# Every second gate and up block by seven products of halves, with the sums of weight halves made by accumulating transfers

## The chip, the cores and the metric

The kernel runs on one core of one Trainium2 chip. The metric is the device time of one execution in microseconds (us); lower is better. In the profile PE is TensorE (matmul), PEld its weight loads, DVE is VectorE, ACT is ScalarE, POOL is GpSimd, and SP is the engine that issues most transfers. A letter q behind an engine's name means its queue of instructions that are no work on data.

## The reference

One inference step of one decoder layer, in float32, for 256 prompt tokens and 8 tokens of running sequences, 264 columns in all. The part that matters here is the feed-forward block, which stands before and after a mixing block:

```python
def swiglu(x, wg, wu, wd):
    return (jax.nn.silu(x @ wg) * (x @ wu)) @ wd

h = h + 0.5 * swiglu(rmsnorm(h, norm_ffn1[l]), ffn1_gate[l], ffn1_up[l], ffn1_down[l])
mix, ... = mixing_block(rmsnorm(h, norm_mix[l]), ...)
h = h + mix
h = h + 0.5 * swiglu(rmsnorm(h, norm_ffn2[l]), ffn2_gate[l], ffn2_up[l], ffn2_down[l])
```

The model width is 2048 (16 tiles of 128 in the contraction), the feed-forward width is 5504 (43 blocks of 128 columns for gate and for up). All weights are read from HBM once.

## The kernel before, in words

**Products in halves of precision.** Activations lie transposed: features on the 128 partitions, the 264 tokens along the free side. Every float32 weight tile `wraw` (eight tiles of 128 by 128, 0.5 MB) is loaded by SP and cut in two float16 parts: ScalarE writes `whi` (line 221, function `high`), VectorE writes the rest `wlo` (line 229, function `low`). Each product of a tile of weights is then three matmuls with 264 columns (lines 288 to 290): high by high, high by low, low by high. A product of a whole block of 128 outputs is `product`: 16 tiles, so 48 matmuls. Inside it stands the order of the work, written out by hand: after every eight tiles the next weight tile is fetched and cut (`fetch`, up to five tiles ahead), then one step of a side schedule runs (`prepare_step`), and `tick` runs what was put on the agenda with `at(delta, ...)`, counted in products. Engines run their instructions in the order in which they are written here.

**The two halves of a feed-forward layer.** `ffn` goes through gate and up for blocks 0 to 21, multiplies them to the activations of the down projection, does the down projection with these blocks, and then the same for blocks 22 to 42. An ordinary block is a gate product, its silu, and an up product.

**Blocks by seven.** Some blocks (list `SEVEN`, 11 in the first layer and 12 in the second, every third one) compute gate and up as one product of two-by-two parts: the weights are cut in gate and up and in the first and second half of the contraction, the input in the halves of the contraction and the two halves of the tokens (132 each). Seven products of 8 tiles do the work of eight (the Winograd form), each as three float16 matmuls with 132 columns (line 410). Three products, with weight halves as they are (tile `sa`, three slots), form the first chunk; four, with sums of weight halves (tile `sb`, four slots), form the second (`chunk_by_seven` with c = 0 and 1). They go to three banks p, q, r; afterwards `by_seven` puts gate and up together from them: ScalarE copies one result (`m`, line 756), VectorE does four additions, a check value and the multiplication with the norm (lines 766 to 774), ScalarE the silu (line 777). The input side, sums of halves of the normed input, is made once a layer by `Norm.form` and `form_split` on ScalarE, POOL and VectorE.

**How the weight sums are made.** `prepare` fills the side schedule `steps`, eight steps a block. POOL issues four loads of 0.5 MB a block into `sraw` (line 332; two buffers, each for half of the tiles). Per buffer ScalarE and VectorE cut three halves to `sa`; VectorE makes the sums `ssum` in three instructions (lines 356 to 358), and ScalarE and VectorE cut these to `sb`. In the order of blocks the second chunk stands one ordinary block behind the first.

**Checks.** `watch` keeps a statistic of each ordinary product (tile `stat`, NSTAT columns) and `twins` one of each block by seven; if one is out of bounds, the whole step is run again in another form of float32.

Of the kernel before, what the change touches and what calls it, by code (L numbers as in the profile page):

```python
# [8 lines left out]
F32 = mybir.dt.float32  # L9
# [29 lines left out]
NSTAT = 320  # L39
# [10 lines left out]
SEVEN = {n: list(range(j, 22, 3)) + list(range(22, NFB, 3)) for n, j in (("1", 10), ("2", 7))}  # L50
# [95 lines left out]
def step(ctx: ExitStack, tc: tile.TileContext, a: dict, shared, bad=None):  # L146
# [171 lines left out]
    def prepare(pool, layer):  # L318

        gu = a[f"w{layer}gu"]
        ks = [slice(0, 4), slice(4, 8)]
        raws = [None, None]
        steps.clear()
        step_no[0] = None

        def load(j, c):
            raws[c] = raw = pool.tile([128, 4, 4, 128], F32, tag="raw", name="sraw", bufs=2)
            for g in range(2):  # L330
                blocks = gu[j, g].rearrange("p (s k) m -> p s k m", s=2)
                queue.dma_start(raw[:, 2 * g : 2 * g + 2], blocks[:, :, ks[c], :])  # L332

        def blocks(j, c):
            if c == 0:
                formed[j, 0] = [
                    pool.tile([128, 3, 8, 128], PART, tag=f"sa{i}", name=f"sa{i}")
                    for i in range(2)
                ]
            high(formed[j, 0][0][:, :, ks[c]], raws[c][:, 0:3], sw)  # L340

        def blocks_low(j, c):
            hi, lo = formed[j, 0]
            low(lo[:, :, ks[c]], raws[c][:, 0:3], hi[:, :, ks[c]], sw)

        sums = [None]

        def all_sums(j, c):
            raw = raws[c]
            if c == 0:  # L350
                formed[j, 1] = [
                    pool.tile([128, 4, 8, 128], PART, tag=f"sb{i}", name=f"sb{i}")
                    for i in range(2)
                ]
            sums[0] = s = pool.tile([128, 4, 4, 128], F32, tag="ssum", name="ssum")
            nc.vector.tensor_tensor(s[:, 2], raw[:, 2], raw[:, 3], op=ALU.add)
            nc.vector.tensor_tensor(s[:, 3], s[:, 2], raw[:, 1], op=ALU.subtract)
            nc.vector.tensor_tensor(  # L358
                s[:, 0:2], raw[:, 0:4:2],
                s[:, 3].unsqueeze(1).to_broadcast([128, 2, 4, 128]), op=ALU.subtract,  # L360
            )
            high(formed[j, 1][0][:, :, ks[c]], s, sw)

        def sums_low(j, c):
            hi, lo = formed[j, 1]
            low(lo[:, :, ks[c]], sums[0], hi[:, :, ks[c]], sw)

        for n, j in enumerate(SEVEN[layer]):
            for s, fn, c in (
                (2, blocks, 0), (3, blocks_low, 0), (3, blocks, 1), (4, blocks_low, 1),  # L370
                (5, all_sums, 0), (6, sums_low, 0), (7, all_sums, 1), (8, sums_low, 1),
            ):
                steps.setdefault(8 * n + s - (3 if n == 0 else 0), []).append((fn, j, c))
            for c in range(2):
                s = -4 if n == 0 else 8 * n + (-2, -1)[c]
                steps.setdefault(s, []).append((load, j, c))

    def prepare_step():
        if step_no[0] is not None and step_no[0] < step_end[0]:
            for fn, j, c in steps.get(step_no[0], ()):  # L380
                fn(j, c)
            step_no[0] += 1

    def chunk_by_seven(j, c, x, forms, banks):
# [7 lines left out]
        def form(n):  # L392
# [4 lines left out]
            (p, 1, lambda k: x[k][:, :, left]), (p, 0, lambda k: x[k + 8][:, :, left]),  # L397
            (r, 0, form(3)),
# [1281 lines left out]
```

## Time and profile before

| | |
|---|---|
| time, median of 3 runs | 1814.26 us (1813.57 to 1816.54) |
| profiled execution, first to last instruction (span) | 1812.0 us |
| TensorE busy | 1796.6 us (99%) |
| VectorE busy | 1391.5 us (77%) |
| ScalarE busy | 958.0 us (53%) |
| GpSimd busy | 250.2 us (14%) |
| transfers | 381.34 MB, mean 210 GB/s |
| mean granted TensorE clock | 0.998 |

The profile comes from one execution. What it gives for that execution is its span; the time outside the span is not shown, and the median of the runs stands 2.3 us above it. A row of a group has the line, the engine, the operation, output and inputs with their shapes, the count, then busy time and mean nanoseconds of one, then the idle time before it and what ended it. Rows of the time line have start, length, engine and line. "Landing" is the time from the issue of a transfer until its data are there.

### The profile page before, as it was taken

Reading aid. Unit: us, or ns where it says so; the run is one execution under the profiler, and the core shown is the slowest. Engines: PE = TensorE matmul, PEld = TensorE weight load, DVE = VectorE, ACT = ScalarE, POOL = GpSimd, SP = SyncE. Lnnn points to the kernel's source line nnn. Section 1 sums busy time; section 2 is a strip of 40 time slices with the busy share of each in tenths; the row PEclk is TensorE's granted clock in tenths of the full one; section 3 lists DMA queues with packets and bytes.
Section 4 is the critical chain, followed back from the end, with each engine's and each line's share of the span. In section 5 each row is a group of like instructions: output and inputs, shape, how many; then the busy total and the mean of one; then the engine's idle time right before and its main releaser. Section 6 shows DMA issues by size and latency. Waiting matters only on the chain.

```text
span 1812.0 us, 42493 instructions
## 1 busy us (share of the span) xinstructions
PE 1796.6 (99%) x17920; PEld 1590.5 (88%) x17920; DVE 1391.5 (77%) x2132; ACT 958.0 (53%) x1329; POOL 250.2 (14%) x339
## 2 busy tenths in 40 slices
PE   9999999999999999999999999999999999999997
PEld 7889988899998888888888888889988889999886
DVE  7888985579997667788888766789986459998554
ACT  7664554445554444667566645655554435554442
POOL 0310000000100222222121022410000001010131
PEclk9999999999999999999999999999999999999999
DMA  9765666645654565988887655756567646564663
GB/s 300 251 219 170 218 225 212 202 157 191 217 189 151 187 190 193 307 279 273 282 282 241 221 179 185 253 191 221 190 187 257 199 147 213 193 209 155 190 193 97
DMA packets 118503, 381.34 MB, mean 210 GB/s; under 512 B 14972, under 2 KB 24796, under 8 KB 118304
## 3 DMA queue, kind: packets, MB, share of 16 engines
q1 hardware_dynamic: 95856, 302.29, 51.1%
q0 software_dynamic: 21504, 75.81, 12.4%
q8 instruction: 142, 2.33, 0.5%
q10 hardware_dynamic: 944, 0.45, 0.1%
q14 instruction: 57, 0.47, 0.1%
HBM read 366.72 MB, written 11.78 MB: 209 GB/s over the span
## 4 chain that ended last, share of the span: by engine, by line
PE 98%; DVE 1%; DMA 0%; ACT 0%; issue 0%; SPq 0%; DVEq 0%; ACTq 0%
PE ps L288 28%; PE ps L290 28%; PE ps L289 28%; PE ps L410 12%; PE ps L506 1%; PE ps L624 0%; PE ps L1349 0%; PE ps L1292 0%; PE ps L1247 0%; DMA wraw<-in_w1gu 0%; DVE sq L698 0%; DVE h L918 0%; PE ps L1270 0%; PE ps L1333 0%; PE ps L1271 0%; ACT whi L221 0%
## 5 line engine op out<-in xcount | busy, mean ns | idle before, releaser
L229 DVE SCALAR_TENSOR_TENSOR wlo<-wraw,whi 128x1024 f16<-128x1024 f32 (+2 forms) x600 | 695.2, 1181 | 97.3 <-ACT whi L221 96.9
L221 ACT ACTIVATE whi<-wraw 128x1024 f16<-128x1024 f32 (+2 forms) x600 | 585.0, 1001 | 202.3 <-PE ps L289 166.8
L290 PE MATMUL ps<-x,wlo 128*128 128x264 f16 x1952 | 539.4, 276 | 0.0
L288 PE MATMUL ps<-x,whi 128*128 128x264 f16 x1952 | 539.4, 276 | 0.0
L289 PE MATMUL ps<-x,whi 128*128 128x264 f16 x1952 | 539.4, 276 | 0.0
L289 PEld LDWEIGHTS <-whi 128*128 128x128 f16 x4522 | 442.2, 98 | 66.4
L288 PEld LDWEIGHTS <-whi 128*128 128x128 f16 x4522 | 442.5, 98 | 65.3 <-issue 0.6
L290 PEld LDWEIGHTS <-wlo 128*128 128x128 f16 x4522 | 442.3, 98 | 65.2
L288 PE MATMUL ps<-a,whi 128*128 128x264 f16 (+2 forms) x1418 | 383.3, 273 | 0.0
L289 PE MATMUL ps<-a,whi 128*128 128x264 f16 (+2 forms) x1418 | 383.3, 273 | 0.0
L290 PE MATMUL ps<-a,wlo 128*128 128x264 f16 (+2 forms) x1418 | 383.2, 273 | 0.0
L288 PE MATMUL ps<-xm,whi 128*128 128x264 f16 x896 | 247.6, 276 | 0.0
L289 PE MATMUL ps<-xm,whi 128*128 128x264 f16 x896 | 247.6, 276 | 0.0
L290 PE MATMUL ps<-xm,wlo 128*128 128x264 f16 x896 | 247.6, 276 | 0.0
L221 ACT ACTIVATE sb<-ssum 128x2048 f16<-128x2048 f32 x46 | 87.9, 1910 | 177.3 <-DVE ssum L358 177.3
L410 PEld LDWEIGHTS <-sb 128*128 128x128 f16 x2208 | 128.8, 98 | 0.7
L860 DVE SCALAR_TENSOR_TENSOR h<-ps,h 128x264 f32<-128x264 f32 x62 | 26.8, 432 | 130.5 <-PE ps L290 130.5
L229 DVE SCALAR_TENSOR_TENSOR sb<-ssum,sb 128x2048 f16<-128x2048 f32 x46 | 105.3, 2289 | 6.0 <-ACT sb L221 3.6
L410 PE MATMUL ps<-f,sb 128*128 128x132 f16 x1656 | 99.0, 221 | 0.0
L410 PEld LDWEIGHTS <-sa 128*128 128x128 f16 x1656 | 97.1, 98 | 0.7
L332 POOL DMA_DIRECT2D sraw<-in_w2gu x48 | 34.6, 722 | 420.3 <-issue 382.0
L332 POOL DMA_DIRECT2D sraw<-in_w1gu x44 | 31.7, 723 | 392.5 <-issue 359.3
(256 smaller groups left out, 1665.9 us busy)
## 6 DMA issues: line engine op xcount, KB each, us to landing
wraw<-in_w2gu SPq DMA_DIRECT2D x124, 512.0 KB, 4.6
wraw<-in_w1gu SPq DMA_DIRECT2D x120, 512.0 KB, 4.9
wraw<-in_win SPq DMA_DIRECT2D x112, 512.0 KB, 5.6
wraw<-in_w1d SPq DMA_DIRECT2D x80, 448.0 KB, 4.1
wraw<-in_w2d SPq DMA_DIRECT2D x80, 448.0 KB, 3.8
sraw<-in_w2gu POOLq DMA_DIRECT2D x48, 512.0 KB, 5.3
sraw<-in_w1gu POOLq DMA_DIRECT2D x44, 512.0 KB, 5.3
wraw<-in_wout SPq DMA_DIRECT2D x32, 512.0 KB, 4.8
```

Of the source, the lines that this page charges most:

```text
L221: nc.scalar.activation(dst, src, AF.Copy, scale=scale)
L229: nc.vector.scalar_tensor_tensor(dst, src, scale, hi, op0=ALU.mult, op1=ALU.subtract)
L288: nc.tensor.matmul(ps, wh, xk[:, 0, :], start=first, stop=False)
L289: nc.tensor.matmul(ps, wh, xk[:, 1, :], start=False, stop=False)
L290: nc.tensor.matmul(ps, wl, xk[:, 0, :], start=False, stop=last)
L332: queue.dma_start(raw[:, 2 * g : 2 * g + 2], blocks[:, :, ks[c], :])
L410: nc.tensor.matmul(out, w[:, f, k, :], b(k)[:, part, :], start=(k + term == 0), stop=(k == 7 and term == 2),)
L506: nc.tensor.matmul(ps[j0 + j], w[:, nk * j + k, :], x[k0 + k][:, part, :], start=(k0 + k + n == 0), stop=(k0 + k == KB - 1 and n == 2),)
L860: nc.vector.scalar_tensor_tensor(h[db], ps, 0.5 / (sw * sa[layer]), h[db], op0=ALU.mult, op1=ALU.add)
```

## The change

1. **More blocks by seven**: every second one, 17 in the first layer (8 to 20, then 22 to 40, in steps of two) and 18 in the second (6 to 20, then 22 to 40), 35 for 23. An ordinary block is between any two of them, and its gate product now stands before the second chunk, its up product behind it.
2. **Sums by transfers**: `ssum` and its VectorE instructions go. The buffer holds three half blocks (1.5 MB): the first half of gate, the second half of gate and the first half of up. After the cuts for the first chunk, POOL issues an accumulating transfer that adds the second half of up to two of these slots (S1 and S2); after the cuts of these, one that adds the second half of gate to S2's slot (S3); after the cut of that, one that adds the first half of gate (S4). Each cut is one instruction on ScalarE and one on VectorE, over one or two slots of 1024 elements.
3. **The rhythm**: six steps of the side schedule a block for eight; one step is now also run at the end of each chunk. In the second chunk the product with S4 comes last. During a down projection no steps run.
4. The form of the sums changes some signs: one more small POOL instruction in `Norm.form`, and by_seven's activations are cut with the opposite sign. `NSTAT` is 288 instead of 320.

```diff
-SEVEN = {n: list(range(j, 22, 3)) + list(range(22, NFB, 3)) for n, j in (("1", 10), ("2", 7))}
+SEVEN = {n: list(range(j, 22, 2)) + list(range(22, NFB - 1, 2)) for n, j in (("1", 8), ("2", 6))}
...
+        def upper(j):
+            raws[j] = raw = pool.tile([128, 3, 8, 128], F32, tag="raw", name="sraw", bufs=2)
+            queue.dma_start(raw[:, 2], gu[j, 1][:, 0:8, :])
+            queue.dma_start(raw[:, 1], gu[j, 0][:, 8:16, :])
+        def lower(j):
+            queue.dma_start(raws[j][:, 0], gu[j, 0][:, 0:8, :])
+        def adds(j, slots, g, s):
+            dst, src = raws[j][:, slots], gu[j, g][:, 8 * s : 8 * s + 8, :]
+            n = slots.stop - slots.start
+            if n > 1:
+                src = src.unsqueeze(1).to_broadcast([128, n, 8, 128])
+            queue.dma_start(dst, src, accum_op=ALU.add)
...
+        def cut(j, c, slots, of):
+            hi, lo = tiles(j, c)
+            high(hi[:, slots], raws[j][:, of], sw)
+        def cut_rest(j, c, slots, of):
+            hi, lo = tiles(j, c)
+            low(lo[:, slots], raws[j][:, of], hi[:, slots], sw)
+        one, two, three_ = slice(0, 1), slice(1, 3), slice(2, 3)
         for n, j in enumerate(SEVEN[layer]):
-            for s, fn, c in (
-                (2, blocks, 0), (3, blocks_low, 0), (3, blocks, 1), (4, blocks_low, 1),
-                (5, all_sums, 0), (6, sums_low, 0), (7, all_sums, 1), (8, sums_low, 1),
+            for s, fn, *what in (
+                (-3, upper), (-2, lower),
+                (0, cut, 0, two, two), (1, cut_rest, 0, two, two), (1, adds, two, 1, 1),
+                (1, cut, 0, one, one), (2, cut_rest, 0, one, one),
+                (4, cut, 1, two, two), (4, cut_rest, 1, two, two), (4, adds, three_, 0, 1),
+                (6, cut, 1, slice(3, 4), three_), (6, cut_rest, 1, slice(3, 4), three_),
+                (6, adds, three_, 0, 0),
+                (8, cut, 1, one, three_), (8, cut_rest, 1, one, three_),
             ):
-                steps.setdefault(8 * n + s - (3 if n == 0 else 0), []).append((fn, j, c))
...
+                steps.setdefault(6 * n + s, []).append((fn, j, *what))
...
             work = (
-                (q, 0, lambda k: x[k][:, :, right]), (q, 2, form(1)), (q, 1, form(0)),
-                (p, 2, form(2)),
-            )
+                (1, q, 2, form(1)), (2, q, 1, form(0)), (3, p, 2, form(2)),
+                (0, q, 0, lambda k: x[k][:, :, right]),
+            )
...
+        prepare_step()
...
-                    elif j - 2 in sevens:
-                        order += [("seven", i - 2, j - 2, 1), ("one", i, j, 0)]
+                    elif j - 1 in sevens:
+                        order += [("gate", i, j, 0), ("seven", i - 1, j - 1, 1), ("up", i, j, 0)]
```

More of the change, by code (lines that the diff above doesn't have):

```diff
@@ L322, in prepare @@
         gu = a[f"w{layer}gu"]
-        ks = [slice(0, 4), slice(4, 8)]
-        raws = [None, None]
+        raws, parts = {}, {}
         steps.clear()
         step_no[0] = None
[L328 to L337, printed above, removed]
+        def upper(j):
+            raws[j] = raw = pool.tile([128, 3, 8, 128], F32, tag="raw", name="sraw", bufs=2)
+            queue.dma_start(raw[:, 2], gu[j, 1][:, 0:8, :])
+            queue.dma_start(raw[:, 1], gu[j, 0][:, 8:16, :])
@@ new lines, in lower, with tiles @@
+        def lower(j):
[6 more added lines that the diff above has]
+            queue.dma_start(dst, src, accum_op=ALU.add)
+        def tiles(j, c):
+            if (j, c) not in formed:
+                formed[j, c] = [
+                    pool.tile([128, 3 + c, 8, 128], PART, tag=f"s{'ab'[c]}{i}", name=f"s{'ab'[c]}{i}")
@@ L821, in ffn @@
                             by_seven(j, i)
+                        continue
+                    if kind != "one":
+                        (gate if kind == "gate" else up)(i, j)
                         continue
```

77 lines of the change are left out of this document (28 added, 49 removed).

## The prediction

> **What bounds the kernel now.** I read the page first (shares of the engines), then the chain of waits that ended last, then one stretch of the gate and up blocks instruction by instruction, then the transfers.
>
> ```profile
> span 1812.0 us, 42493 instructions
> PE 1796.6 (99%) x17920; PEld 1590.5 (88%) x17920; DVE 1391.5 (77%) x2132; ACT 958.0 (53%) x1329; POOL 250.2 (14%) x339
> PE 98%; DVE 1%; DMA 0%; ACT 0%; issue 0%; SPq 0%; DVEq 0%; ACTq 0%
> ```
>
> TensorE carries 98% of the chain: less matmul work is less time, as long as nothing else makes it wait. The chain in order of time (start, length) gives the prices; x72 is the first chunk of a block by seven, x96 its second.
>
> ```profile
> 391.93 4.14 PE ps L410 x72
> 406.87 5.52 PE ps L410 x96
> 423.19 4.14 PE ps L410 x72
> ```
>
> Between the end of a first chunk (391.93 + 4.14 = 396.07) and the second (406.87) lies one ordinary block: 10.80 us, so 5.40 for its gate and 5.40 for its up product. A block by seven costs 4.14 + 5.52 = 9.66 us; one of its products is 5.52 / 4 = 1.38. Each of the twelve blocks that change kind (23 become 35) saves 1.14 us of TensorE: **-13.7 us** in all. That is the whole gain.
>
> The same three blocks as a window (busy time of each engine, granted clock, DMA share, GB/s), and the end of the run:
>
> ```profile
> core 0: us, PE busy (x) PEld busy (x) DVE busy (x) ACT busy (x) POOL busy (x), PEclk, DMA share, GB/s
> 391.93:423.19 31.26, 31.26 (x363) 28.44 (x361) 28.55 (x39) 16.63 (x20) 2.88 (x5) 1.00 0.61 203
> ...
> 1800.00:1812.00 12.00, 0.95 (x12) 0.62 (x12) 4.50 (x14) 0.91 (x4) 0.00 (x0) 0.64 0.42 120
> ```
>
> TensorE has no gap there, VectorE is at 28.55 / 31.26 = 91%, ScalarE at 53%, the DMA engines at 61%.
>
> **What stays beside other work.**
>
> ```profile
> L229 DVE SCALAR_TENSOR_TENSOR wlo<-wraw,whi 128x1024 f16<-128x1024 f32 x420 | 509.5, 1229 | 51.9 <-ACT whi L221 51.7
> L358 DVE TENSOR_TENSOR ssum<-sraw,ssum 128x1024 f32<-128x1024 f32 x46 | 56.3, 1225 | 1.6
> L357 DVE TENSOR_TENSOR ssum<-ssum,sraw 128x512 f32<-128x512 f32 x46 | 31.8, 692 | 1.6
> L356 DVE TENSOR_TENSOR ssum<-sraw 128x512 f32<-128x512 f32 x46 | 31.5, 686 | 0.0
> L664 POOL TENSOR_TENSOR form_t<-form_b x16: 732/747/1385, 46.3 to 1174.6; 128x264 f32<-128x264 f32 x16
> L666 POOL TENSOR_TENSOR form_t<-form_t,form_b x16: 462/960/1329, 47.6 to 1178.0; 128x132 f32<-128x132 f32 x16
> ```
>
> The three sums leave VectorE: 56.3 + 31.8 + 31.5 = 120 us, none of it on the chain, so worth nothing by itself. In the new rhythm, one block by seven and one ordinary block (10.80 + 9.66 = 20.46 us; a "pair" below), VectorE has the old 28.55 less 2 x (1.225 + 0.692 + 0.686) = 5.2 of sums and less about 7 for the ordinary block that goes (four cuts of 1.23 and some 2 us around them): 16.3 of 20.46, 80%. It gets lighter, ScalarE hardly changes, neither becomes the bound. The input forms are now made one a product instead of one in 1.25 to 1.5; their POOL work, 0.75 + 0.96 + two small ones, stays under 4 us in 5.40: hidden, nothing. The negated sign, the smaller statistics tile and the halves of an ordinary block as two calls cost no instruction.
>
> POOL now issues six transfers for a block by seven instead of four, and three of these wait for VectorE. Behind a waiting one, only the loads of the next blocks queue. Bytes for a pair: four ordinary tiles, three half blocks loaded and four added, eleven times 0.5 MB, 5.8 MB in 20.46 us, or 282 GB/s against 203.
>
> **What lies on the path.** The sums S3 and S4 are made in place: the transfer for S3 may start only when VectorE has finished its cut of S2 from the same bytes, that for S4 only when S3 is cut. So per block two accumulating transfers, two hops to POOL and three cuts stand in series, and the first cut is behind the previous block's end. These rows price that series (first ScalarE, VectorE and POOL in order of time, then two summaries):
>
> ```profile
> 407.37 1.47 ACT L221 ACTIVATE sa<-sraw 128x1536 f16<-128x1536 f32 x1
> 408.74 1.04 ACT L221 ACTIVATE whi<-wraw 128x1024 f16<-128x1024 f32 x1
> 409.69 1.47 ACT L221 ACTIVATE sa<-sraw 128x1536 f16<-128x1536 f32 x1
> ...
> 412.42 0.27 ACT L756 COPY m<-ps 128x132 f32<-128x132 f32 x1 [0.52 <-PE ps L410]
> 415.23 0.42 ACT L777 ACTIVATE tb<-y 128x264 f32<-128x264 f32 x1 [2.53 <-DVE y L774]
> 415.55 1.99 ACT L221 ACTIVATE whi<-wraw 128x1024 f16<-128x1024 f32 x2
> 421.75 1.91 ACT L221 ACTIVATE sb<-ssum 128x2048 f16<-128x2048 f32 x1 [4.21 <-DVE ssum L358]
> ```
>
> ```profile
> 389.17 1.22 DVE L358 TENSOR_TENSOR ssum<-sraw,ssum 128x1024 f32<-128x1024 f32 x1
> ...
> 408.87 1.76 DVE L229 SCALAR_TENSOR_TENSOR sa<-sraw,sa 128x1536 f16<-128x1536 f32 x1
> 413.19 0.43 DVE L767 TENSOR_TENSOR y<-ps,y 128x264 f32<-128x264 f32 x1
> 422.34 1.22 DVE L229 SCALAR_TENSOR_TENSOR wlo<-wraw,whi 128x1024 f16<-128x1024 f32 x1
> 423.70 2.29 DVE L229 SCALAR_TENSOR_TENSOR sb<-ssum,sb 128x2048 f16<-128x2048 f32 x1
> ...
> 390.95 1.44 POOL L332 DMA_DIRECT2D sraw<-in_w1gu  x2 [130.47 <-issue]
> 398.94 1.44 POOL L332 DMA_DIRECT2D sraw<-in_w1gu  x2 [6.55 <-issue]
> ```
>
> ```profile
> sraw<-in_w1gu POOLq DMA_DIRECT2D x44, 512.0 KB, 5.3
> cs<-in_c POOLq DMA_DIRECT2D x16, 512.0 KB, 5.9
> out_c_s<-cs POOLq DMA_DIRECT2D x16, 512.0 KB, 5.1
> DMA to landing us min/median/max: 4.3/5.3/12.3
> DMA to landing us min/median/max: 3.2/5.3/8.9
> GB/s 63 189 267 356 383 414 325 231 231 194 47 204 241 398 414 325 346 89 31 173 341 189 215 225 273 273 278 47 0 0 0 0 68 231 309 84 136 267 252 16
> ```
>
> The two landing rows are those of sraw and of cs, 0.5 MB each from POOL. I now follow one turn of the loop, with zero at the end of a second chunk E (412.39 in the rows).
>
> - The result of the block: in the new order its last product touches only one bank, so the copy m and the first of VectorE's sums can go before E. VectorE's second sum (413.19) starts about 0.1 after E, and the silu follows it as in the rows, 415.23 - 413.19 = 2.04 later: silu at 2.1.
> - ScalarE works in program order: silu to next start 0.32 (415.55 - 415.23), a weight cut 0.95 (409.69 - 408.74), then the cut of S1 and S2, which has the size of the sb row, 1.91: ends at 5.3.
> - VectorE's rest of it, 0.04 later as in the rows (421.75 + 1.91 = 423.66, then 423.70), 2.29: 7.6.
> - POOL issues the transfer 0.56 after VectorE ends (389.17 + 1.22 = 390.39, then 390.95): 8.2. It lands L later.
> - S3: cut 1.04 and rest 0.04 + 1.22, hop 0.56, transfer L. S4: cut 1.04, rest 0.04 + 1.22.
>
> Together 8.2 + 2.86 + 2.30 = 13.4, plus 2 L. TensorE wants S4 for the last product of the next second chunk, which without a stall starts at 5.40 (up) + 4.14 (first chunk) + 5.40 (gate) + 3 x 1.38 = 19.08. (That it waits for the slot alone and not the whole tile, I take from the rows: at 409.69 ScalarE writes the second half of sa while VectorE still reads the first, 408.87 to 410.63.) **The stall of a pair is 2 L - 5.7**; the loop has slack only for L under 2.85 us.
>
> L for an accumulating transfer of 0.5 MB is not in the trace. The nearest row is sraw: same queue, bytes and direction, median 5.3, fastest 4.3; the fastest transfer of that size into or out of cs, also from POOL, is 3.2. Reading the destination too adds something between nothing and another whole transfer (out_c_s, which reads such a tile out of the same memory, 5.1): 10.4. I stay near sraw: one more pass of 0.5 MB at the best rate of the row (414 GB/s) is 1.3 us, and half of it is 0.65, because the engines may overlap it: L = 5.9, between 5.3 and 6.6. The stall is then 6.1 us a pair.
>
> It does not come in every pair. After each first half the down projection lets the sums catch up, so 16 of 17 pairs in the first layer and 17 of 18 in the second pay; the first pair of a layer follows no result by seven and pays some 1.5 less. 33 x 6.1 - 3 = **+198 us**.
>
> The clock: in the last 12 us above TensorE has 0.95 us of work and the mean clock is 0.64; if it falls from 1 to 0.5 after t, t + 0.5 (12 - t) = 7.7 gives t = 3.4 us, with almost no work in them. A stall of 6 us is longer. At half clock the last product takes 1.38 more; what comes behind it has the slack of the stall. So between 0 and 33 x 1.38 = 45; I take the middle, **+23**, as no row shows how soon the clock returns. The Trainium skill ("TensorE: Matmul & The Clock Gate", Part 1) says that an idle window of some 3.4 us halves the clock until a busy window has passed; the drop at the end agrees, no run here shows the return, and by that rule the sum would take the whole 45.
>
> Sum against the profiled execution's span of 1812.0: -13.7 + 198 + 23 = +207, 2019 us; the median of the runs is 2.3 above that span, so 2021, and I say **2020**.
>
> **The rivals.**
>
> *The loop closes in time* (faster). Decides at L under 2.85 us. Then only -13.7 is left: 1800.6. For it: the DMA engines are at 61% and some loads on the other queue are quick. Against: no 0.5 MB from POOL landed in under 3.2, and these carry extra work. 0.07.
>
> *The fixed cost rules L*: each lands as the fastest transfer of cs, 3.2; the stall is 0.7, 33 x 0.7 - 3 - 13.7 = +6, 1821. The median rows speak against it. 0.08 up to 1840. The Trainium skill ("DMA: Bandwidth & Descriptors", "Anatomy of one DMA — SWDGE (gpsimd) path") has about 2.0 us plus bytes over 436 GB/s, which for 0.5 MB is 3.2 as an estimate; the fastest cs agrees, the median of sraw, 5.3, does not.
>
> *The DMA engines are the bound.* If an added byte counts twice, a pair is 5.8 + 2.1 = 7.9 MB. At the window's own rate, 203 / 0.61 = 333 GB/s, that is 23.6 us, 3.2 over 20.46: 35 x 3.2 - 13.7 = +98, 1912. For it: 282 GB/s is above the present mean. Against: bursts of 414, at which it would be 19.0 and fit; and the loop above is longer anyhow. 0.07.
>
> *TensorE waits for the whole tile of sums* at the chunk's start: the loop is 13.4 + 5.52 + 2 L against 20.46, the stall 2 L - 1.5 = 10.3, 33 x 10.3 - 3 + 23 - 13.7 = +346, 2160. The bank of m hints at it (the copy waited until E for a slot finished one chunk earlier); the overlapping halves of sa speak against. 0.08.
>
> **How the numbers follow.** The loop with slots and L from 4.3 to 8 has 0.70: by the same formula L = 4.3 gives a stall of 2.9, +79 without the clock, 1893; L = 7.9 (two more passes, 5.3 + 2.6) gives 10.1 and with the whole clock +362, 2176. The range 1850 to 2180 takes in the DMA rival and the whole-tile one at 5.9; outside are the faster case, the 3.2 case and L beyond 8. A measurement here can tell about 0.2% (3.6 us) from no change. Faster 0.07, within 0.2% 0.03 (L just around 2.9 to 3.1), slower 0.90.
>
> **What the new profile would show.** TensorE's chunks of 4.14 and the first three quarters of the second as before, then a gap of about 6 us ahead of the last quarter, released by VectorE's rest of S4; ScalarE waiting for a transfer into sraw twice a pair; POOL's accumulating issues 0.56 after VectorE; a pair at some 27 us instead of 20.46; PEclk under 1.00 in these windows; down projection and mixing block unchanged. Wrong if TensorE has no gap in second chunks, if the transfers land in under 3 us, if the gap stands at the chunk's start (whole tile), or if it is spread over ordinary weight tiles (DMA bound).

## The result

The changed kernel takes 2106.14 us (median of 4 runs, 2104.65 to 2108.55) against 1813.91 (4 runs, 1813.34 to 1816.54): ratio 1.1613, 95% interval 1.1596 to 1.1629. The profiled execution's span is 2106.7 us against 1812.0, so +294.7. The page of the changed kernel (in its rows the matmuls by seven have line 403 for 410, the copy `m` 753 for 756, the accumulating transfers 340, a block's loads 329, 330 and 333):

```profile
span 2106.7 us, 44342 instructions
PE 1876.8 (89%) x18784; PEld 1653.6 (78%) x18784; DVE 1339.2 (64%) x2053; ACT 1004.2 (48%) x1376; POOL 363.5 (17%) x473
PEclk9988889998888999999999999888889998988999
PE 40%; DMA 26%; issue 12%; DVE 11%; ACT 8%; POOL 1%; DVEq 0%; SPq 0%; ACTq 0%; POOLq 0%
```

TensorE's share of the chain fell from 98% to 40%; transfers, VectorE and ScalarE took its place, and TensorE, still the busiest engine, is at 89%. What TensorE waited for (total us, times, longest), in the view of waits:

```profile
PE ps L403 <- ACT sb L221: 172.3, 36, 7.2
PE ps L403 <- DVE sb L229: 37.3, 42, 2.0
```

That is 210 us, all ahead of parts of `sb`, the sums; ordinary weight tiles do not appear. The windows place it by stage:

```profile
core 0: us, PE busy (x) PEld busy (x) DVE busy (x) ACT busy (x) POOL busy (x), PEclk, DMA share, GB/s
90.00:330.00 240.00, 191.97 (x2085) 170.83 (x2084) 146.28 (x193) 106.75 (x122) 39.47 (x52) 0.88 0.78 212
430.00:706.00 276.00, 220.10 (x2577) 198.36 (x2575) 162.27 (x212) 113.17 (x129) 40.65 (x52) 0.88 0.75 190
330.00:430.00 100.00, 100.00 (x891) 86.97 (x890) 50.14 (x66) 40.83 (x42) 0.00 (x0) 1.00 0.63 202
706.00:1300.00 594.00, 592.28 (x5208) 513.61 (x5209) 444.67 (x811) 341.37 (x586) 126.07 (x179) 1.00 0.69 229
```

The down projection (330 to 430) and the mixing block (706 to 1300) keep TensorE busy all but 1.7 us, at clock 1.00. The stages with blocks by seven have TensorE busy 80% of the time at clock 0.88. One pair in the time line, of PE, ACT, DVE and POOL:

```profile
1491.79 4.30 PE L403 MATMUL ps<-f,sb 128*128 128x132 f16 x72
1492.86 0.85 POOL L340 DMA_DIRECT2D sraw<-in_w2gu  x1 [7.36 <-DVE sb L229]
1493.61 2.28 DVE L229 SCALAR_TENSOR_TENSOR sa<-sraw,sa 128x2048 f16<-128x2048 f32 x1
...
1496.20 1.19 POOL L340 DMA_DIRECT2D sraw<-in_w2gu  x1 [2.48 <-DVE sa L229]
1498.79 1.06 ACT L221 ACTIVATE sb<-sraw 128x1024 f16<-128x1024 f32 x1 [2.85 <-DMA sraw<-in_w2gu]
1499.90 0.40 PE L403 MATMUL ps<-x,sb 128*128 128x132 f16 x2 [3.81 <-ACT sb L221]
...
1501.16 2.60 PE L403 MATMUL ps<-x,sb 128*128 128x132 f16 x22 [0.86 <-DVE sb L229]
...
1507.86 1.91 ACT L221 ACTIVATE sb<-sraw 128x2048 f16<-128x2048 f32 x1 [0.62 <-DMA sraw<-in_w2gu]
1509.80 2.29 DVE L229 SCALAR_TENSOR_TENSOR sb<-sraw,sb 128x2048 f16<-128x2048 f32 x1 [2.90 <-ACT sb L221]
1512.39 0.87 POOL L340 DMA_DIRECT2D sraw<-in_w2gu  x1 [9.83 <-DVE sb L229]
```

Three quarters of the second chunk (x72) run, then TensorE stands for 3.81 us until ScalarE has cut S4 (1498.79), runs two matmuls, and waits again, 0.86 us, for VectorE's rest. The gap is where the prediction put it. Below, A1, A2 and A3 are a block's three accumulating transfers in order: here A3 of one block (1492.86), A1 of the next (1496.20) and its A2 (1512.39). The chain of waits through the same pair:

```profile
1484.07 6.15 DMA sraw<-in_w2gu
...
1490.24 1.07 ACT sb L221
...
1492.47 0.69 DVE wlo L229
...
1493.61 2.29 DVE sa L229
...
1496.20 11.56 DMA sraw<-in_w2gu
...
1507.86 1.92 ACT sb L221
...
1509.80 2.31 DVE sb L229
...
1512.39 6.13 DMA sraw<-in_w2gu
```

No TensorE is in it. From one A2 (1484.07) to the next (1512.39) are 28.32 us: the landing of A2, the cut of S3, the rests that stand behind it in VectorE's order, the next block's A1 with 11.56, the cut of S1 and S2, A2 again. This is a second closed loop, and the prediction did not have it.

A1 in the second layer (median landing at the end of the row), the landing of all accumulating transfers, large and small (minimum, median, maximum), and GpSimd's queue as a share of 16 engines:

```profile
sraw<-in_w2gu POOLq DMA_DIRECT2D x18, 1024.0 KB, 10.4
DMA to landing us min/median/max: 5.5/6.4/12.0
q0 software_dynamic: 42976, 156.03, 31.2%
```

### The profile page after: what moved, and what is told of

It reads as the page before. It is cut to its first block, busy times and chain, and to the rows that moved or that the text cites. A ratio compares the mean times of both kernels' runs of the same rounds, so it can differ in the third digit from the quotient of the medians.

```text
span 2106.7 us, 44342 instructions
## 1 busy us (share of the span) xinstructions
PE 1876.8 (89%) x18784; PEld 1653.6 (78%) x18784; DVE 1339.2 (64%) x2053; ACT 1004.2 (48%) x1376; POOL 363.5 (17%) x473
## 3 DMA queue, kind: packets, MB, share of 16 engines
q0 software_dynamic: 42976, 156.03, 31.2%
## 4 chain that ended last, share of the span: by engine, by line
PE 40%; DMA 26%; issue 12%; DVE 11%; ACT 8%; POOL 1%; DVEq 0%; SPq 0%; ACTq 0%; POOLq 0%
DMA sraw<-in_w2gu 14%; PE ps L288 12%; PE ps L289 12%; PE ps L290 12%; DMA sraw<-in_w1gu 12%; ACT sb L221 4%; DVE sb L229 4%; DVE sa L229 3%; ACT whi L221 2%; DVE wlo L229 1%; ACT sa L221 1%; PE ps L403 1%; DMA wraw<-in_w1gu 1%; PE ps L500 1%; DVE y L771 1%
## 5 line engine op out<-in xcount | busy, mean ns | idle before, releaser
L229 DVE SCALAR_TENSOR_TENSOR wlo<-wraw,whi 128x1024 f16<-128x1024 f32 (+2 forms) x552 | 634.2, 1178 | 156.5 <-ACT whi L221 155.8
L288 PEld LDWEIGHTS <-whi 128*128 128x128 f16 x4138 | 412.0, 100 | 64.8 <-issue 0.6
L289 PEld LDWEIGHTS <-whi 128*128 128x128 f16 x4138 | 411.2, 99 | 65.4 <-issue 0.3
L288 PE MATMUL ps<-x,whi 128*128 128x264 f16 x1568 | 450.3, 287 | 0.0
L289 PE MATMUL ps<-x,whi 128*128 128x264 f16 x1568 | 448.4, 286 | 0.0
L290 PE MATMUL ps<-x,wlo 128*128 128x264 f16 x1568 | 446.6, 285 | 0.0
L403 PEld LDWEIGHTS <-sb 128*128 128x128 f16 x3360 | 235.7, 110 | 228.0 <-ACT sb L221 178.9
L229 DVE SCALAR_TENSOR_TENSOR sb<-sraw,sb 128x1024 f16<-128x1024 f32 (+1 forms) x105 | 166.0, 1581 | 299.9 <-ACT sb L221 299.9
L403 PE MATMUL ps<-x,sb 128*128 128x132 f16 x840 | 101.8, 309 | 192.3 <-ACT sb L221 163.6
L221 ACT ACTIVATE sb<-sraw 128x1024 f16<-128x1024 f32 (+1 forms) x105 | 140.6, 1339 | 261.2 <-DMA sraw<-in_w2gu 132.8
L403 PE MATMUL ps<-f,sb 128*128 128x132 f16 x2520 | 157.5, 224 | 17.4 <-DVE sb L229 8.7
L403 PEld LDWEIGHTS <-sa 128*128 128x128 f16 x2520 | 147.7, 98 | 3.4 <-DVE sa L229 2.3
## 6 DMA issues: line engine op xcount, KB each, us to landing
sraw<-in_w2gu POOLq DMA_DIRECT2D x18, 1024.0 KB, 10.4
```

The source lines that it names most:

```text
L221: nc.scalar.activation(dst, src, AF.Copy, scale=scale)
L229: nc.vector.scalar_tensor_tensor(dst, src, scale, hi, op0=ALU.mult, op1=ALU.subtract)
L288: nc.tensor.matmul(ps, wh, xk[:, 0, :], start=first, stop=False)
L289: nc.tensor.matmul(ps, wh, xk[:, 1, :], start=False, stop=False)
L290: nc.tensor.matmul(ps, wl, xk[:, 0, :], start=False, stop=last)
L403: nc.tensor.matmul(out, w[:, f, k, :], b(k)[:, part, :], start=(k + term == 0), stop=(k == 7 and term == 2),)
```

## The experiments

Between two copies `m`, that is from one result by seven to the next, the kernel before takes 31.26 us (three blocks, "a triple"), the changed one 28.93 in the mean of 31 (two blocks, "a pair"; 20.46 without a gap). This distance is the measure in what follows. The ratios are to the kernel before.

**1. Every third block again, sums still by transfers.** `SEVEN` as before; ten steps a block, and the chain of a block laid wholly behind that of the block before.

```diff
-                (-3, upper), (-2, lower),
-                (0, cut, 0, two, two), (1, cut_rest, 0, two, two), (1, adds, two, 1, 1),
+                (-6, upper), (-5, lower),
+                (-3, cut, 0, two, two), (-2, cut_rest, 0, two, two), (-2, adds, two, 1, 1),
...
-                (6, adds, three_, 0, 0),
-                (8, cut, 1, one, three_), (8, cut_rest, 1, one, three_),
+                (4, adds, three_, 0, 0),
+                (7, cut, 1, one, three_), (7, cut_rest, 1, one, three_),
```

> The sums stay accumulating transfers, with the same bytes and the same in-place order for a block, but the blocks by seven go back to every third one (23 of them) and the chain of a block is spread over the ten steps that three blocks have (first transfer three steps, second three, third three before its use). Theory 1 (the loop of dependent transfers is too long for the rhythm): three blocks last 31.3 us, more than the loop's 28, so TensorE has no gaps and the time is that of the kernel before, 1810 to 1818. Theory 2 (the DMA engines are the bound): eight ordinary tiles, three loads and four added half blocks in 31.3 us, at the rates of the changed kernel about 0.65 of the engines, also no gaps: 1810 to 1820. Theory 3 (an accumulating transfer costs time wherever it stands, through POOL or memory): 23/35 of the loss stays, about +200, 2010.

Measured: 1983.18 us (1982.32 to 1989.43), ratio 1.0946 (1.0928 to 1.0964); a triple 38.29. The expectation of no gaps missed. With this step table the series A1, A2, A3 and the next block's cuts follow one another in a circle of 38 us, so the longer rhythm alone does not help: what counts is which steps close a circle. The next block's plain loads are in it too: in one turn they are issued from 1442.18 on, behind A3 (1441.43) on the same queue, and ScalarE waits for them:

```profile
1453.94 1.91 ACT L221 ACTIVATE sa<-sraw 128x2048 f16<-128x2048 f32 x1 [5.08 <-DMA sraw<-in_w2gu]
```

**2. The same order, nothing added.** The transfers write instead of adding, so the sums are left out (and layer 2's activations are scaled to a quarter). Same bytes from HBM, same waits.

```diff
-            queue.dma_start(dst, src, accum_op=ALU.add)
+            queue.dma_start(dst, src)
```

> The changed kernel with plain transfers in place of the accumulating ones: same bytes, same places, same waits, but the half blocks are overwritten instead of added, so the sums are left out; the activations of the second layer are cut with a quarter of the scale, so that they stay in range. Theory 1: the loops keep their form and only the landings get shorter, 0.5 MB from 6.1 to about 5 and 1 MB from 11.5 to about 7; the loop over two small transfers is then 12.9 + 2 x 5 + 1.4 to 2.6 = 24.3 to 25.5 us for a pair against 20.5, so TensorE still waits 4 to 5 us a pair: 1930 to 1970, slower than before even with no addition in any transfer. Theory 2: the added bytes count once instead of 1.9 times, the engines fall well under their limit, all gaps go: about 1800.

Measured: 1979.76 us (1978.33 to 1981.18), ratio 1.0915 (1.0894 to 1.0937); a pair 25.51. The rows of its transfers:

```profile
DMA to landing us min/median/max: 3.8/4.7/8.6
sraw<-in_w2gu POOLq DMA_DIRECT2D x18, 1024.0 KB, 7.6
```

166 of the 292 us are lost though nothing is added (10 us more than the upper end of what was expected): more than half of the loss is the series of steps, not the addition in the transfers. With L = 4.7 the prediction's formula gives a pair of 13.4 + 9.4 + 1.38 = 24.2; in the first half of the first layer the pairs are 24.1 to 24.8, and there the chain of waits is the predicted loop, without A1: A2 and A3 with 4.2 to 4.8 us each, the cuts of S3 and S4, the result, the silu, the cut of S1 and S2.

**3. A1 sooner.** The next block's cut of S1 and S2 and its A1 go to the front of their step, ahead of the cut of S3 and of A3 of the block before.

```diff
+            steps[6 * n] = [
+                (cut, j, 0, two, two), (cut_rest, j, 0, two, two), (adds, j, two, 1, 1)
+            ] + steps.get(6 * n, [])
```

> Only the order of a step is changed: the cut of the next block's two slots, its rest and the 1 MB transfer stand ahead of the cut of S3, so that this transfer leaves about 5 us sooner. Theory 1 with two loops: the loop first transfer, second transfer, next first transfer (28.3 us) is broken, and the loop from the end of one second chunk over two 0.5 MB transfers to the next is left, 12.9 + 2 x 6.1 + 2.6 = 27.7 us a pair instead of a mean of 28.9: 33 x 1.2 = 40 less, 2055 to 2080. Theory 1 with one loop only (the one that was predicted): no change, 2100 to 2110. Theory 2: no change either, the bytes are the same.

Measured: 2285.2 us (2282.87 to 2287.54), ratio 1.26 (1.2574 to 1.2625); a pair 33.78. Wrong side. The time line shows why:

```profile
1596.95 1.20 POOL L340 DMA_DIRECT2D sraw<-in_w2gu  x1 [5.53 <-DVE sa L229]
...
1598.65 0.89 POOL L340 DMA_DIRECT2D sraw<-in_w2gu  x1 [0.50 <-DVE sb L229]
...
1610.10 1.06 ACT L221 ACTIVATE sb<-sraw 128x1024 f16<-128x1024 f32 x1 [8.58 <-DMA sraw<-in_w2gu]
```

A3 (1598.65) is issued 1.70 behind A1 on the same queue and its cut starts 11.45 later, where A3 took 5.93 in the changed kernel (1492.86 to 1498.79). A3 lies in the loop that TensorE waits for, and a turn of that loop is 32.97 us in this pair (from A2 at 1589.99 to A2 at 1622.96). The time line does not show when A1 itself landed, and the DMA engines are full meanwhile (share 0.94 to 1.04 in the windows from 1599 to 1610), so how much of the 11.45 is the place behind A1 and how much the full engines is not shown. The Trainium skill ("DMA: Bandwidth & Descriptors", "Queues, rings and completion order") has each DMA engine take turns between the queues that it has work for. That A3 gained no turn of its own beside A1, on the same queue, would agree with it, but this run does not separate the two.

**4. The same with the gap filled**, to hold the clock: 88 matmuls more ahead of the last product, whose result is overwritten.

```diff
+            for i in range(88 if c == 1 and n == 3 and j != 22 else 0):
+                nc.tensor.matmul(
+                    out, hi[:, 1, i % 8, :], form(1)(i % 8)[:, 0, :], start=True, stop=True
+                )
```

> As the run before (first transfer sooner), and TensorE works through the wait: 88 matmuls of 132 columns (5.1 us) into the place that the last product of the second chunk then overwrites; their results are not used. Theory clock: the gap falls under a microsecond or two, the granted clock stays at 1.0, the last product takes 1.4 instead of 2.6 us, and as it is in the loop each of 33 pairs gets 1.2 us shorter: 40 less than the run before, although TensorE has more to do. Theory no clock: the added work only fills the wait, same as the run before within 10; or the time goes up where the work outlasts the wait.

Measured: 2290.4 us (2287.34 to 2293.45), ratio 1.2628 (1.2603 to 1.2653), not told apart from run 3; the mean clock went from 0.903 to 0.941 and the time not at all.

**5. S4 on VectorE.** The first loop loses a transfer: VectorE adds the first half of gate, which is still in the buffer.

```diff
-                (6, adds, three_, 0, 0),
+                (6, plus, 0),
```

> The changed kernel, but S4 is made by VectorE (one addition of 1024 elements in place, about 1.2 us) instead of the third transfer. This takes one of the two 0.5 MB transfers out of the loop that was predicted: that loop falls to 12.6 + 1.2 + 6.1 + 1.4 to 2.6 = 21.3 to 22.5 us a pair. Theory with one loop: 33 x 6.4 less, about 1890. Theory with two loops: the other one (1 MB transfer, cut, 0.5 MB transfer, cut, next 1 MB transfer: 28.3 us) does not contain this transfer, and the addition on VectorE stands in it, so the pair stays at 28 to 29.5 us: 2070 to 2120, no gain although a transfer has gone.

Measured: 2083.35 us (2081.81 to 2084.9), ratio 1.1472 (1.1448 to 1.1495); a pair 28.28, the length of the second loop in the chain (28.32). The loop on which the prediction rests was shortened by some 5 us and almost nothing came of it: the second loop alone holds the pair.

**6. Both, 3 and 5 together.**

> Both edits: S4 by VectorE and the 1 MB transfer ahead of the cut of S3. Theory with two loops: each edit alone does little, together they break both; what is left is from the end of a first chunk over the 1 MB and one 0.5 MB transfer to the next second chunk, 31.9 us against 30.0 that there are, so 2 us a pair: 20.5 + 2 = 22.5, 1860 to 1900. If the DMA engines are the next bound (seven plain half blocks at 3.0 and three added ones at 5.6 engine-us a MB: 19.6 of 22.5 us), it ends at the upper side, up to 1930.

Measured: 1956.45 us (1955.7 to 1957.19), ratio 1.0773 (1.0751 to 1.0794); a pair 24.47, 4.5 less than in the changed kernel. Each edit alone gained 23 us or lost 179; together they gain 150. So there are two loops, and only the cut of both shows. (That the first loop alone would hold the pair at nearly the same length no run shows by itself, since run 3 made it longer by A3; its length is read from rows further down.) 24.47 is 2 above what I expected, and the time lies above the upper side of 1930; what holds the pair there this run does not show.

**7. Two small transfers a block.** VectorE makes two of the four sums; transfers of 0.5 MB make the other two; A1 with its 1 MB is gone.

```diff
+                (0, adds, three_, 1, 1),
...
+                (4, cut, 1, three_, three_), (4, cut_rest, 1, three_, three_), (4, plus, 1),
+                (4, adds, slice(1, 2), 1, 1),
+                (5, cut, 1, slice(3, 4), three_), (5, cut_rest, 1, slice(3, 4), three_),
+                (5, plus, 0),
```

> A rearrangement in the same rhythm (35 blocks): S2 and S1 by one accumulating transfer of 0.5 MB each, S3 and S4 by VectorE in place, the product with S1 last in the second chunk. No chain over two transfers is left: S2's transfer leaves after the first chunk and lands about when the second ends; S1's leaves about 7 us after the second chunk's end and lands at 13.5, before its use at about 19 less 2.3 for the cuts. VectorE has 18.8 of 20.5 us (92%). Theory 1: TensorE has no gaps, the predicted gain of 12 x 1.14 us comes in full: 1798 to 1805, faster than the kernel before. If VectorE at 92% or landings under load (more than 9 us) make gaps: 1810 to 1850. Theory 3 (accumulating transfers cost wherever they stand): above 1850.

Measured: 1952.09 us (1951.25 to 1955.09), ratio 1.0747 (1.0729 to 1.0765); pairs of 23.70 in the first halves and 25.6 in the second, nearly without spread. The expectation missed. One pair of a first half as a window, and what VectorE waited for:

```profile
1391.82:1415.53 23.71, 20.80 (x256) 18.66 (x255) 19.92 (x26) 12.28 (x15) 3.32 (x5) 0.95 0.68 197
DVE wlo L229 <- ACT whi L221: 120.2, 121, 3.4
DVE sb L229 <- ACT sb L221: 65.4, 68, 1.4
```

VectorE is busy 19.92 us, 97% of the 20.46 that the pair should take, and it also waits for ScalarE at each cut. Here no transfer is the bound; the order of cuts, sums and results on two engines is. Why the second halves need 1.9 more stays open.

**8. Every third block, chain spread.** As 1, but the first cuts and A1 of a block stand ahead of the cut of S4 of the block before, and A3 has a step more on either side.

```diff
-                (-3, cut, 0, two, two), (-2, cut_rest, 0, two, two), (-2, adds, two, 1, 1),
-                (-2, cut, 0, one, one), (-1, cut_rest, 0, one, one),
+                (-4, cut, 0, two, two), (-4, cut_rest, 0, two, two), (-4, adds, two, 1, 1),
+                (-3, cut, 0, one, one), (-3, cut_rest, 0, one, one),
...
-                (4, cut, 1, slice(3, 4), three_), (4, cut_rest, 1, slice(3, 4), three_),
-                (4, adds, three_, 0, 0),
-                (7, cut, 1, one, three_), (7, cut_rest, 1, one, three_),
+                (5, cut, 1, slice(3, 4), three_), (5, cut_rest, 1, slice(3, 4), three_),
+                (5, adds, three_, 0, 0),
+                (8, cut, 1, one, three_), (8, cut_rest, 1, one, three_),
```

> Every third block again, sums by the same accumulating transfers, but the steps are laid out so that the next block's first cut and first transfer stand ahead of this block's S4, and the two small transfers have four and three steps. In the first run with every third block the chain of one block (8.6 + 4.3 + 6.2 + 2.6 + 6.4 us and the cuts between) stood wholly behind that of the block before, 38 us against 31.3. Theory 1 (loops of dependent transfers): now two blocks' chains overlap, each transfer has its landing time and TensorE has no gaps: 1812 to 1830. Theory 3 (an accumulating transfer costs wherever it stands): about as the first run, 1950 to 1990. In between if a wait is left: a gap of 1 us a block is 21 us.

Measured: 1892.26 us (1887.87 to 1896.51), ratio 1.042 (1.0396 to 1.0443); a triple 34.53. The expected 1812 to 1830 was missed, but with the same transfers as in 1 the loss fell from 170 to 78 us. The rest shows a new place, in ScalarE's rows:

```profile
1309.93 0.87 POOL L340 DMA_DIRECT2D sraw<-in_w2gu  x1 [6.88 <-DVE sb L229]
1310.48 0.86 POOL L333 DMA_DIRECT2D sraw<-in_w2gu  x1
...
1319.79 1.06 ACT L221 ACTIVATE sa<-sraw 128x1024 f16<-128x1024 f32 x1 [3.67 <-DMA sraw<-in_w2gu]
...
1321.69 1.04 ACT L221 ACTIVATE sb<-sraw 128x1024 f16<-128x1024 f32 x1
```

The plain load of line 333 is issued behind A3 and lands 9.3 us later; ScalarE waits for it, and the cut of S4 stands behind that cut in its order.

**9. The changed kernel with the gap filled.** The edit of 4 on the changed kernel.

> The changed kernel itself with TensorE kept at work in the wait ahead of the last product of the second chunk (88 matmuls of 132 columns, whose results the product then overwrites). Theory clock in the loop (as predicted, up to 1.4 us a pair): 2106 - 33 x 1.2 = 2065. Theory second loop (1 MB transfer, cut, 0.5 MB transfer, cut, next 1 MB transfer, none of it on TensorE): the granted clock goes up, but the time stays, 2090 to 2115.

Measured: 2088.1 us (2087.14 to 2089.07), ratio 1.1507 (1.1484 to 1.153). The mean clock rises from 0.933 to 0.987 and the time falls by 18 us, a little below the 2090 expected for the second loop. That is what the half clock cost: 0.3 us a pair (28.61 for 28.93) and some 2 us at each of the four starts of a half.

**10 and 11. No accumulating transfers.** All four halves are loaded and the sums are made on chip: in 10 three by GpSimd and one by VectorE, in 11 all by GpSimd.

```diff
+        def plus(j, engine, slot, other):
+            to, by = (part(j, slice(i, i + 1)) for i in (slot, other))
+            engine.tensor_tensor(to, to, by, op=ALU.add)
...
+                (0, plus, side, 2, 3), (0, plus, side, 3, 1),
...
+                (4, plus, nc.vector, 2, 1),
...
+                (5, plus, side, 2, 0),
```

These lines are of 10 (`side` is GpSimd); in 11 the third sum is `side` too.

> The new rhythm (35 blocks by seven, 6 steps) with no accumulating transfer: the fourth half block is loaded too, S1, S2 and S4 are made by POOL in place and S3 by VectorE; the second chunk takes S2, S1, S3, S4 in this order, and the weight tiles have five raw buffers instead of six. Theory 1: no transfer waits for a cut any more, so what is left is the engines' own program: VectorE 17.3 + 1.2 = 18.5 of 20.5 us. If its waits for ScalarE fit in the rest, no gaps: 1800 to 1815, faster than the kernel before. If not (the run with two accumulating transfers had 19.9 us of VectorE work in pairs of 23.7 to 25.6), pairs of 22 to 23: 1850 to 1900. POOL's additions of 1024 elements are not in any row; from 0.46 us for 132 and 0.73 for 264 elements an estimate is 2.3 us, up to 5 when VectorE is busy.

> As the run before, with S3 on POOL too: VectorE 17.3 of 20.5 us, but S3 lies in the series from the end of one second chunk to the last product of the next: about 19.3 us against 19.1 that there are, with additions of 2.3 us each; with 4 us each 22.7, a stall of 3.6. If VectorE's program is what binds: below the run before, 1800 to 1820. If the series with POOL binds: above it, 1810 to 1930.

Measured: 10 takes 2113.23 us (2109.87 to 2116.53), ratio 1.1646 (1.1623 to 1.1669), a pair 28.74; 11 takes 2166.39 (2165.32 to 2171.25), ratio 1.1937 (1.1917 to 1.1957), a pair 30.38. Both missed. GpSimd's sums in 10, and VectorE's:

```profile
L346 POOL TENSOR_TENSOR sraw<-sraw,slast 128x1024 f32<-128x1024 f32 x35 | 112.6, 3217 | 427.1 <-DVE sa L229 418.0 <-DMA slast<-in_w2gu 5.1 <-DMA slast<-in_w1gu 3.9
L346 POOL TENSOR_TENSOR sraw<-sraw 128x1024 f32<-128x1024 f32 x35 | 82.1, 2345 | 424.0 <-DVE sb L229 424.0
L346 DVE TENSOR_TENSOR sraw<-sraw 128x1024 f32<-128x1024 f32 x35 | 42.9, 1225 | 1.2
```

A sum of 1024 elements takes GpSimd 2.3 to 3.2 us, VectorE 1.2. These steps are shorter than the 6.1 and 11.5 us of the transfers, and yet the time is no better. In both runs TensorE still waits for the cuts of sums, 177 us of it for VectorE's in run 10: the sums in place, each behind the cut of the one before, stay a series whoever makes them. And GpSimd's sums make VectorE's work longer. In one pair of run 10, where TensorE waits 4.56 us for the second of these rows:

```profile
1464.30 3.25 POOL L346 TENSOR_TENSOR sraw<-sraw,slast 128x1024 f32<-128x1024 f32 x1 [4.88 <-DVE sa L229]
1465.27 3.37 DVE L229 SCALAR_TENSOR_TENSOR sb<-sraw,sb 128x1024 f16<-128x1024 f32 x1
```

The cut of 1024 elements takes VectorE 3.37 us for 1.22; it ends 1.09 after GpSimd's sum, as if it had run behind that sum and not beside it. Over run 10 three groups of VectorE's rows grow like this against the changed kernel: the cuts to `sb` (mean 1.89 for 1.23, 105 of them), those of one slot to `sa` (2.32 for 1.22, 35) and the gate's multiplication `tc` (1.81 for 0.43, 51), together 179 us or 5.1 a pair, where the pair is 8.3 over 20.46. So the sums on GpSimd were not beside other work; how much each part cost was not separated.

**12. As 8, loads sooner.** The three loads of a block go ahead of A3 of the block before on GpSimd's queue.

```diff
-                (-6, upper), (-5, lower),
+                (-9 if n else -6, upper), (-9 if n else -5, lower),
```

> The same 23 blocks and the same spread chain as in the run before with every third block (1892.26), but the three loads of a block are issued three steps sooner (step -9 for -6 and -5, but for the first block of a layer), so that they stand on GpSimd's queue behind the second accumulating transfer of the block before and no longer behind the third, and the cut of the slot that the late load brought no longer holds up ScalarE. If that late load is the rest of the loss, the gap before the last product goes: a triple at 31.3 to 32 us for 34 to 36, and 1812 to 1840 in all, about the time of the kernel with sums on VectorE. If the series from S3's cut through the last transfer to S4's cut is itself too long for its place, or the transfers slow each other when the loads move beside them, triples stay at 34 us or more and the time at 1870 to 1900.

Measured: 1858.88 us (1858.56 to 1859.92) against 1816.03 for the kernel before beside it, ratio 1.0243 (1.0226 to 1.0261); a triple 32.77. Between the two expectations: the late load cost some 35 of the 78 us. TensorE's waits for sums are 28 us, for 210 in the changed kernel:

```profile
PE ps L403 <- ACT sb L221: 14.4, 9, 5.4
PE ps L403 <- DVE sb L229: 13.3, 15, 2.1
```

Of the 43 us that are left, 19 triples have (32.77 - 31.26) each, 29 us, and the first block of the second layer, which comes 13.7 us later than in the kernel before (656.5 against 642.8 between the layers' results), nearly all the rest. What holds the triples at 32.77 stays open. No version ran faster than the kernel before.

## Why the prediction was right, step by step, and where its sizes were off

**The saving, -13.7.** Nothing speaks against it, and nothing shows it by itself: TensorE's busy time rose by 80 us, as matmuls at half clock last longer.

**The first loop** (E, A2, A3, the next E). It is there as written, but it is not what sets the pair. From E (1501.16 + 2.60 = 1503.76) to A2 (1512.39) are 8.6 us for 8.2 predicted (the hop from VectorE to GpSimd is 0.29, 1512.11 to 1512.39, for 0.56), and 0.62 of them are ScalarE's wait for A1 (the row at 1507.86), which the prediction did not have. The small transfers took 6.13 (A2) and 5.93 (A3) for L = 5.9. By the formula with 6.1 the pair is 13.4 + 12.2 + 1.38 = 27.0; by the rows, with the last product at half clock, the loop is 28.32 less that wait, 27.7. The longer part of TensorE's gap ended with ScalarE's cut of S4, not, as predicted, with VectorE's rest.

**What was mis-sized: the stall of a pair**, 8.5 us (28.93 - 20.46) for 6.1. The term that failed is "the first cut is behind the previous block's end" together with L as the only unknown transfer: the sum counted A2 and A3 and took A1, twice as large, as off the path. A1 took 11.56 and closes a loop of 28.3 of its own, since A1 of the next block stands behind the cut of S3 in the order of ScalarE and VectorE. The second loop is 0.6 longer than the first in the pair shown; runs 5 and 6 show that it holds the pair, the one by shortening the first loop with little effect, the other by breaking both. The remainder up to 28.93 is half clock (0.3, run 9) and spread: single pairs run from 27.7 to 31.3. TensorE's own waits, 210 us or 6.0 a block, look like the predicted 6.1, but that is chance: the rest of the 8.5 stands in matmuls at half clock, and these do not set the length (28.61 with the clock held, run 9).

**L as "one more pass at the best rate".** Right in size for 0.5 MB, by luck: without addition the small transfers took 4.2 to 4.8 (run 2, first half of the first layer) for 5.3 assumed, and the addition cost more than the 0.65 that was put on top. At 414 GB/s the further 0.5 MB of A1 would be 1.3 us and its addition as much again; from 6.1 for 0.5 MB to 11.56 for 1 MB are 5.4, in a stretch in which the DMA engines are full (share 0.95 to 1.06 in the windows below). The prediction did not price the 1 MB transfer at all.

**The first pair of a layer.** "Pays some 1.5 less" was wrong in sign. Its whole series begins only at its first chunk, and nothing of it was done before. The first rows of the changed kernel's first layer (A1, A2, A3, then the cut of S4):

```profile
97.99 1.26 POOL L340 DMA_DIRECT2D sraw<-in_w1gu  x1 [3.36 <-DVE sa L229]
...
112.86 0.87 POOL L340 DMA_DIRECT2D sraw<-in_w1gu  x1 [12.49 <-DVE sb L229]
...
121.70 0.86 POOL L340 DMA_DIRECT2D sraw<-in_w1gu  x1 [7.42 <-DVE sb L229]
...
127.79 1.06 ACT L221 ACTIVATE sb<-sraw 128x1024 f16<-128x1024 f32 x1 [3.01 <-DMA sraw<-in_w1gu]
```

From A1 to the end of the cut are 30.9 us. The first result stands at 131.95; in the kernel before it stands at 137.32 with two and a half ordinary blocks (27.0 us) more ahead of it, so about 22 us are lost here, and by the same count 18 at the start of the second layer.

**The clock, +23 between 0 and 45.** Run 9 puts it at 18. The restart shows in the pair above: 22 matmuls in 2.60 us, and in the window that follows the granted clock is 0.50 until 1505.8 and then full, 4.6 us after the work resumed at 1501.16:

```profile
1499.90:1503.80 3.90, 3.04 (x26) 2.70 (x27) 3.20 (x5) 0.58 (x2) 1.15 (x2) 0.50 1.03 236
1503.80:1505.80 2.00, 2.00 (x11) 1.38 (x10) 1.90 (x6) 0.00 (x0) 0.00 (x0) 0.50 1.06 250
1505.80:1510.10 4.30, 4.30 (x39) 3.73 (x38) 1.40 (x2) 3.61 (x4) 0.00 (x0) 0.99 0.95 344
1491.00:1519.50 28.50, 23.83 (x272) 21.33 (x270) 17.32 (x23) 12.61 (x15) 4.62 (x6) 0.88 0.78 202
```

The Trainium skill ("TensorE: Matmul & The Clock Gate", Part 1) lets a busy window of some 3.4 us give the full clock back; 4.6 here is of that order. That the whole 45 would be paid is not what the runs show: with the clock held, a pair was 28.61 for 28.93 (run 9), and the second loop has no TensorE in it.

**The sum.** 31 distances of 8.5, 263; the two first pairs, 40; the two first pairs behind a down projection, 1.7 each (141.0 for 139.3); less 13.7: +293, measured +294.7. The prediction's +207 had 73 too little in the pairs, some 31 in the first pairs and 3 at the down projection, and 23 of clock that is part of the measured stall. The time lies inside the stated range, but the range was made wide for a longer L and for the rivals; it took in a second loop and two costly starts that nobody had priced.

**VectorE lighter, no bound.** Half right. A pair has 17.32 us of VectorE (last row above) for 16.3 predicted. It binds nowhere in the changed kernel, but in run 7, with two sums back on it, it does.

**The rivals.** *The DMA engines are the bound*, 1912: not what holds the pair here. Run 2 keeps the bytes read and more than half of the loss with a share of 0.67 in its pairs, ordinary tiles have no wait worth a line, and the share in the changed kernel is 0.75 to 0.78 in the windows. But the rival's price was near: 28.5 us at 0.78 (last row above) are 22.2 us of all 16 engines for a pair, for 23.6 predicted, and more than the 20.46 that a pair should take. As an estimate from this share, and if it cannot be made smaller, these transfers would cost 31 x 1.74 = 54 us without any loop, against the 13.7 to be gained; no run here shows that. The engines also have a part in the second loop, as they are full while A1 is under way. *TensorE waits for the whole tile*: refuted by the rows, the x72 run first. *The fixed cost rules L*, 3.2: no accumulating transfer landed in under 5.5. *The loop closes in time*: it misses by 8.5 us; for every second block the same series would also miss with plain transfers (run 2).

## What to carry to other kernels

When a sum is moved from an engine into a transfer in place, count the closed circles that its waits make with the order of instructions on each engine and queue, and price every transfer in them by its size; the longest circle is the rhythm, and shortening another shows little. Then add up the DMA engines' time for one turn, with the added bytes at their own price; here it was 22.2 us for a turn of 20.46. The sums were 5.2 us a block of VectorE's time beside other work, and became a gap of 8.5 us a pair. Look at the first turn too: a loop that is tight in its rhythm has no head start there and pays the whole series once.

## What the runs showed of the hardware that was not expected

- An accumulating transfer runs at a low rate beside other traffic (DMA share 0.95 to 1.06 in the windows above): in the pair shown 0.5 MB landed in 6.1 us and 1 MB in 11.56, 5.4 us for the further 0.5 MB, about 97 GB/s; the median for 1 MB in that layer was 10.4, and 7.6 without addition (run 2). In engine time: GpSimd's queue took 224.7 us of 16 engines for 75.81 MB before (2.96 us a MB) and 657.3 for 156.03 after; with the plain loads at 2.96, the 73.4 MB that are added took 5.6 us a MB, 1.9 times as much. Without the addition the same 156.03 MB took 24.0% of 1979.2 us, 475 us, or 3.04 a MB (run 2).
- A transfer of 0.5 MB issued 1.7 us behind one of 1 MB on GpSimd's queue landed after 11.45 us for 5.93, with the DMA engines full (run 3).
- TensorE began the product with S4 on the high parts as soon as ScalarE had them (two matmuls at 1499.90) and waited for VectorE's rest at the third, 0.86 us.
- VectorE's cut of 1024 elements took 3.37 us for 1.22 while GpSimd summed two float32 tiles of 1024 elements, and ended 1.09 us after the sum (run 10).
